# Start of a two-layer encoder trunk: the first token half loaded ahead of the rest, its squares summed by TensorE, and rows of 1/sqrt made without diagonals

## The chip, the cores and the metric

The kernel runs on one core of a Trainium2 chip. The metric is the device time of one execution in microseconds (us), the median of several runs. Engines are named as in the profile: PE (TensorE matmul), PEld (its weight loads), DVE (VectorE), ACT (ScalarE), POOL (GpSimd), SP (SyncE, which only issues transfers). A q behind a name is that engine's instruction queue.

## What is computed

Two layers of a hybrid encoder on 1024 tokens of 1024 channels, in float32:

```python
def rmsnorm(x, g):
    y = x * lax.rsqrt(jnp.mean(x * x, axis=-1, keepdims=True) + EPS)
    return y * g

for l in range(DEPTH):                                  # DEPTH = 2
    h = rmsnorm(x, attn_norm_g[l])
    x = x + hybrid_mixer(h, w_in[l], b_in[l], ...)      # z = h @ w_in + b_in; three branches, gates, w_out
    h = rmsnorm(x, ffn_norm_g[l])
    x = x + conv_ffn(h, w_up[l], ffn_conv_w[l], w_down[l])
return rmsnorm(x, final_norm_g)
```

The change touches the five rmsnorms (two in each layer and the last), the first one above all.

## The kernel before

Channels lie on the 128 partitions, tokens on the free axis. x is held as 8 channel tiles; the 1024 tokens are cut in two halves of 512 (h = 0, 1). Four transfers of 512 KB bring one half: transfer j brings channel tiles j and j + 4 (`x_load`). The input is x_i_0_0 to x_i_0_3 (first half) and x_i_1_0 to x_i_1_3 (second half).

The float32 products are made of float32r matmuls. Each operand is split into a high part (a cast, on ACT) and a low part (a subtraction, on DVE), and three matmuls make one product: high by high, weights' high by activations' low, weights' low by activations' high (`mms`, L336). Weights come as `raw` tiles of 256 KB with five buffers, and their two parts lie in `split` tiles (L286 on ACT, L287 on DVE).

Pairs of output tiles and both token halves make a 2 by 2 block product with one product saved (class `Block`). What this needs: B11 and B21 are the split parts of the normalised first half, T1 to T4 are sums and differences of both halves, s1 to s4 sums of weight quarters that accumulating transfers of the POOL queue make in DRAM-to-SBUF adds. `first` of a block needs the first half alone; `second` needs T2, and so the second half. `start_phase` runs `first` of four blocks, among which the second half's norm is made, then T2, then `second` of the four. So each phase (m_0 and m_1 for the mixers of layers 0 and 1, f_0 and f_1 for their FFNs) begins with the first half's norm.

An rmsnorm of a half: ACT squares each tile of x, DVE adds the eight squares up, PE sums over the partitions with four matmuls against a column of ones (`st`, one column for each 128 tokens), DVE makes the variance (`var`), POOL its power of -0.5 (`rs`, tokens on partitions, four columns). To have this as a row on all partitions, DVE splits it in a high and a low part (`rp`), multiplies the identity by each column (`dg`, two times 128x512), and PE multiplies ones by the two diagonals (`r`, two matmuls of 512 columns). DVE then multiplies x by the norm's weight and by r, eight times 128x512 (L479).

The order on each engine isn't that of the source. A scheduling layer orders the instructions with estimated times and sets the waits on semaphores. A transfer issued by SP or ACT signals one of eight semaphores, DMAHW0 to DMAHW7, given out in turn; before an issuing queue issues a transfer it waits until the transfer that had that semaphore before has landed, so at most eight are under way. `tc.issue_after(i)` keeps what is issued inside it behind instruction i. Before, SP alone issues all plain loads, in this order: four tiles of x's first half, the parameters (`par`, 195 KB), raw_0 to raw_2, four tiles of the second half, s2 of four blocks, raw_3 on.

Of the kernel before, what the change touches and what calls it, by code (L numbers as in the profile page):

```python
# [10 lines left out]
AF = mybir.ActivationFunctionType  # L11
ALU = mybir.AluOpType

P = 128
# [3 lines left out]
H = 512  # L18
NH = S // H
DB = 768  # L20
# [10 lines left out]
NB = H // BLK  # L31
# [70 lines left out]
def encoder(ctx: ExitStack, tc: tile.TileContext, xt, wts, par, bs, wst, cnt, out):  # L102
    nc = tc.nc
# [9 lines left out]
    def slot(name):  # L113

        return up.tile([P, 2, H], F32R, tag="u", name=name)
# [5 lines left out]
    def temp(name):  # L121
        return wp.tile([P, H], F32, tag="t", name=name, bufs=N_TT)
# [4 lines left out]
    def half(h):  # L127
        return slice(h * H, (h + 1) * H)

    parts = [const.tile([P, N_PAR], F32, name=f"par_{l}") for l in range(L)]  # L130
    ones = const.tile([P, P], F32, name="ones")
    nc.gpsimd.memset(ones, 1.0)
    ones_r = const.tile([P, P], F32R, name="ones_r")
    nc.vector.tensor_copy(ones_r, ones)
    ident = const.tile([P, P], F32, name="ident")
# [49 lines left out]
    raws, sums, split = {}, {}, {}  # L185
    state = {"raw": 0, "split": 0, "used": 0, "dma": None, "credit": 0, "pow": None}

    def load_to(n):
        while state["raw"] < min(n, len(raw_units)):
            i = state["raw"]  # L190
            l, t, c0, c1 = raw_units[i]
            w = wp.tile([P, H], F32, tag="raw", name=f"raw_{i}", bufs=N_RAW)
            ins = nc.sync.dma_start(w[:, : c1 - c0], wts[l, t, :, c0:c1])
            state["dma"] = ins.ins
            raws[i] = (w, c1 - c0)
            state["raw"] += 1

    def reload(dst, src):

        with tc.issue_after(state["dma"]):  # L200
            nc.sync.dma_start(dst, src)
# [47 lines left out]
    for l in range(L):  # L249
        plan_blocks(l, [in_tiles(*b) for b in IN_BLOCKS])  # L250
        for i in range(4):
            t, n = T_MIX + i // 2, NPP // 2 * P
# [90 lines left out]
    def halves(u, f):  # L343

        nc.scalar.copy(u[:, 0], f)  # L345
        nc.vector.tensor_tensor(u[:, 1], f, u[:, 0].bitcast(F32), op=ALU.subtract)
# [14 lines left out]
    def add(o, a, b, op=ALU.add):  # L361
        nc.vector.tensor_tensor(o, a, b, op=op)  # L362
# [45 lines left out]
            return run  # L408


    def rsqrt_sums(ss, c0, nc_, n, name):

        nb = nc_ // P
        st = pst.tile([P, H], F32, tag="st", name=f"st_{name}")
        for b in range(nb):
            nc.tensor.matmul(
                st[:, b : b + 1], ss[:, c0 + b * P : c0 + (b + 1) * P], ones[:, 0:1],
                start=True, stop=True,
            )
        var = sm.tile([P, NB], F32, tag="var", name=f"var_{name}")  # L420
        nc.vector.tensor_scalar(var[:, :nb], st[:, :nb], 1.0 / n, EPS, op0=ALU.mult, op1=ALU.add)
        rs = sm.tile([P, NB], F32, tag="rs", name=f"rs_{name}")
        state["pow"] = nc.gpsimd.tensor_tensor(
            rs[:, :nb], var[:, :nb], mhalf[:, :nb], op=ALU.pow
        ).ins
        rp = sm.tile([P, 2, NB], F32R, tag="rp", name=f"rp_{name}")
        nc.vector.tensor_copy(rp[:, 0, :nb], rs[:, :nb])
        nc.vector.tensor_tensor(
            rp[:, 1, :nb], rs[:, :nb], rp[:, 0, :nb].bitcast(F32), op=ALU.subtract
        )  # L430
        dg = wp.tile([P, 2, H], F32R, tag="dg", name=f"dg_{name}", bufs=1)
        for j in range(2):
            nc.vector.tensor_tensor(
                dg[:, j, :nc_].rearrange("p (b t) -> p b t", t=P),
                ident[:, None, :].broadcast_to([P, nb, P]),
                rp[:, j, :nb].bitcast(F32)[:, :, None].broadcast_to([P, nb, P]),
                op=ALU.mult,
            )
        return dg, nc_

    def rsqrt_rows(parts_of, name):

        dg, nc_ = parts_of
        r = pst.tile([P, H], F32, tag="st", name=f"r_{name}")
        for j in range(2):
            nc.tensor.matmul(r[:, :nc_], ones_r, dg[:, j, :nc_], start=j == 0, stop=j == 1)
        return r


    x_dram = [dp.tile([P, KD, S], F32, name=f"x_{i}") for i in range(2 * L)]  # L450

    def x_load(src, h, name, gated=True):

        xq = []
        for j in range(4):
            t = up.tile([P, 2, H], F32, tag="u", name=f"x_{name}_{j}")
            s = src[:, j::4, half(h)]
            if gated:
                reload(t, s)
            else:  # L460
                nc.sync.dma_start(t, s)
            xq.append(t)
        return xq

    def x_part(xq, k):
        return xq[k % 4][:, k // 4]

    def square(sq, xq, k, cols, name):

        s = temp(f"sq_{name}_{k}")  # L470
        nc.scalar.activation(s[:, cols], x_part(xq, k)[:, cols], AF.Square)
        if sq is None:
            return s
        add(sq[:, cols], sq[:, cols], s[:, cols])
        return sq
# [20 lines left out]
    def start_phase(l, col, x0, x1, sq1, name, ops, blocks, late):  # L496
# [3 lines left out]
        for b in blocks[:at]:  # L500
            b.first()
        rows = rsqrt_sums(sq1, 0, H, D, f"{name}_1")
        blocks[at].first()
        r = rsqrt_rows(rows, f"{name}_1")
        for b in blocks[at + 1 :]:
            b.first()
# [214 lines left out]
    def mixer_out(l, d, x_src, x_dst):  # L721
        pr = parts[l]
        tag = f"{l}"
        ws, q = layer[l]

        def col(c):
            return pr[:, c : c + 1]
# [11 lines left out]
        def mix_weights(n):  # L739
            t, at = n // per, n % per * P  # L740
            key = (l, T_MIX + t, at // H * H)
            if key not in wm:
                wm[key] = operand("raw", key)
            return wm[key], at % H

        for m in range(KB):
# [3 lines left out]
            for h in range(NH):  # L750
                ps = pm.tile([P, H], F32, tag="mm", name=f"mix_{tag}_{m}_{h}")
                for n in mine:
                    w, at = mix_weights(n)
# [65 lines left out]
        conv, squares = [], []  # L819
# [27 lines left out]
        def conv_norm():  # L847
            for h in range(NH):
                sl = half(h)
                dg = rsqrt_sums(squares[h], 0, H, DB, f"c_{tag}_{h}")  # L850
                yield
                r = rsqrt_rows(dg, f"c_{tag}_{h}")
                for i in range(KB):
                    c = conv[i][:, sl]
                    nc.vector.tensor_tensor(c, c, r, op=ALU.mult)
                    s = temp(f"csg_{tag}_{h}_{i}")
                    nc.scalar.activation(
                        s, c, AF.Sigmoid, bias=col(C_CLB + i), scale=col(C_CLG + i)
                    )
                    nc.scalar.activation(  # L860
                        c, c, AF.Identity, bias=col(C_CLB + i), scale=col(C_CLG + i)
                    )
                    nc.vector.tensor_tensor(c, c, s, op=ALU.mult)
                    a[h][i] = slot(f"a_{tag}_{h}_{i}")
                    halves(a[h][i], c)
                    yield
# [31 lines left out]
        branch(2, mixed, PUMP[1])  # L898
        drain()
        background.append(conv_norm())  # L900
        branch(1, us, PUMP[2])
        drain()
        branch(0, a, 0)

        def out_half(h, hook):
            xq = x_load(x_src, h, f"o_{l}_{h}")
            sq = None
            for m in range(KD):
                ps = pm.tile([P, H], F32, tag="mm", name=f"po_{tag}_{m}_{h}")
                for j in range(2):  # L910
                    w = operand("raw", (l, T_OUT + m, j * H))
                    mms(ps, w, y[h][j * 4 : j * 4 + 4], j == 0, j == 1)
                xm = x_part(xq, m)
                add(xm, ps, xm)
                nc.sync.dma_start(x_dst[:, m, half(h)], xm)
                sq = square(sq, xq, m, slice(0, H), f"f_{l}_{h}")
                if m == 0 and hook is not None:
                    hook()
            return xq, sq

        x0, sq0 = out_half(0, None)
# [5 lines left out]
        x1, sq1 = out_half(1, hook)  # L927
        return x0, x1, sq1, ops

    def first_half(l, col, x0, sq0, name):  # L930
        normed(x0, rsqrt_rows(rsqrt_sums(sq0, 0, H, D, f"{name}_0"), f"{name}_0"), l, col)
        return first_operands(x0, name)
# [137 lines left out]
            nc.sync.dma_start(out[:, k : k + each, h * H + cols.start : h * H + cols.stop], fv)  # L1070


    x0 = x_load(xt, 0, "i_0", gated=False)
    nc.sync.dma_start(parts[0], par[0])
    load_to(3)
    x1 = x_load(xt, 1, "i_1", gated=False)
    warm = sm.tile([P, 1], F32, tag="warm", name="warm", bufs=1)
    nc.scalar.activation(warm, ones[:, 0:1], AF.Sigmoid)
    sq0 = sq1 = None
    for k in range(KD):  # L1080
        sq0 = square(sq0, x0, k % 2 * 4 + k // 2, slice(0, H), "m_0_0")
    ops = first_half(0, C_NG, x0, sq0, "m_0")
    for k in range(KD):
        sq1 = square(sq1, x1, k % 2 * 4 + k // 2, slice(0, H), "m_0_1")
# [3 lines left out]
    for l in range(L):  # L1088
        x_src = xt if l == 0 else x_dram[2 * l - 1]
        d = mixer_in(l, x0, x1, sq1, ops)  # L1090
        x0, x1, sq1, ops = mixer_out(l, d, x_src, x_dram[2 * l])
        if l + 1 < L:
            x0, x1, sq1, ops = ffn(l, x0, x1, sq1, ops, x_dram[2 * l], x_dram[2 * l + 1])
# [96 lines left out]
```

## Time and profile before

| | |
|---|---|
| median of 3 runs | 2747.4 us (2745.45 to 2749.69) |
| profiled execution, its own time | 2748.52 us |
| its span in the profile | 2746.8 us |
| granted TensorE clock, mean | 0.996 |
| PE busy | 2682.3 us (98% of the span) |
| DVE, ACT, POOL busy | 2057.0, 1255.1, 359.1 us |
| on the chain that ended last | PE 80%, "issue" 7%, DVE 6%, transfers 4%, ACT 1% |

A row of the timeline gives the start in us, the time until the end of the last of its instructions, engine, source line, operation, out<-in, how many instructions, and in brackets the idle time of that engine before it with what ended it. A row of a waits view names who waited for whom: us in total, times, longest. Rows of a windows view give busy us of each engine in one stretch. Tile names there have no numbers: x_i is either half, sq_m its squares. One float32 matmul of the source shows as two rows on PE, a float32r one as one.

### The profile page before, as it was taken

What the parts mean: (1) busy time and instruction counts of PE and PEld (TensorE: products, weight loads), DVE (VectorE), ACT (ScalarE), POOL (GpSimd) and SP (SyncE); (2) the same over time, 40 slices, a digit from 0 to 9 for tenths busy, and PEclk for the clock granted to TensorE, in tenths of its full rate; (3) what the DMA queues carried; (4) which work ended last, traced back from release to release, by engine and by line L of the source; (5) the groups of instructions that cost most, each with busy time, mean ns of one, the idle gap of its engine ahead of it and who ended that gap; (6) DMA issues with size and microseconds to landing.
All of it is one profiled execution on the core that took longest, in us unless ns stands there. A gap on an engine that the chain in (4) does not pass through costs nothing.

```text
span 2746.8 us, 35054 instructions
## 1 busy us (share of the span) xinstructions
PE 2682.3 (98%) x12122; PEld 2209.9 (80%) x12122; DVE 2057.0 (75%) x2899; ACT 1255.1 (46%) x2059; POOL 359.1 (13%) x411
## 2 busy tenths in 40 slices
PE   6999999999999999999999999999999999999998
PEld 4887888878888788878888878888778887888788
DVE  7978879967756876674589789899586579666656
ACT  5654444443333555453365444444352336445534
POOL 2212111100001221100122111110000022211000
PEclk9999999999999999999999999999999999999999
DMA  8887787675357787655568777875634677774654
GB/s 236 200 207 190 206 225 197 185 265 174 112 182 203 169 207 178 172 200 199 150 152 213 195 210 213 217 198 193 230 125 137 205 188 182 198 179 121 215 177 138
DMA packets 272003, 517.92 MB, mean 189 GB/s; under 512 B 28496, under 2 KB 49744, under 8 KB 271824
## 3 DMA queue, kind: packets, MB, share of 16 engines
q1 hardware_dynamic: 217200, 415.51, 45.4%
q0 software_dynamic: 54624, 100.16, 22.2%
q8 instruction: 95, 1.56, 0.2%
q14 instruction: 84, 0.69, 0.1%
HBM read 385.54 MB, written 89.13 MB: 173 GB/s over the span
## 4 chain that ended last, share of the span: by engine, by line
PE 80%; issue 7%; DVE 6%; DMA 4%; ACT 1%; POOL 0%; SPq 0%; DVEq 0%; POOLq 0%; ACTq 0%
PE run_up L336 12%; PE pd L336 12%; PE run_gate L336 10%; PE c_up L336 9%; PE ph L336 9%; PE c_gate L336 7%; PE po L336 4%; PE run_glu L336 4%; PE c_glu L336 3%; DVE conv L590 2%; PE run_v L336 2%; PE c_v L336 2%; PE run_zp L336 1%; DMA poold<-pooled 1%; PE mix L336 1%
## 5 line engine op out<-in xcount | busy, mean ns | idle before, releaser
L286 ACT CAST split<-raw 128x512 fp32r<-128x512 f32 (+1 forms) x570 | 342.8, 603 | 474.2 <-PE ph L336 155.6
L287 DVE TENSOR_TENSOR split<-raw,split 128x512 fp32r<-128x512 f32 (+1 forms) x570 | 376.5, 664 | 226.5 <-ACT split L286 222.9
L590 DVE SCALAR_TENSOR_TENSOR conv<-z_glu,par,conv 128x1023 f32<-128x1023 f32 (+9 forms) x360 | 451.8, 1262 | 10.4 <-ACT conv L588 8.3
L286 ACT CAST split<-s 128x512 fp32r<-128x512 f32 x344 | 213.4, 622 | 352.7 <-issue 115.2
L336 PE MATMUL pd<-h,split 128*128 128x512 f32 (+1 forms) x1536 | 314.2, 363 | 3.4 <-ACT split L286 1.5
L336 PEld LDWEIGHTS pd<-h,split 128*128 128x128 f32 x1536 | 262.0, 188 | 51.1 <-ACT h L358 3.0
L287 DVE TENSOR_TENSOR split<-s,split 128x512 fp32r<-128x512 f32 x344 | 234.7, 685 | 71.2 <-ACT split L286 70.4
L218 POOL DMA_DIRECT2D s<-in_wts_dram x220 | 204.5, 968 | 427.7 <-DMA s<-in_wts_dram 202.3
L218 POOL DMA_DIRECT2D s<-s x156 | 135.7, 870 | 762.3 <-DMA s<-in_wts_dram 366.0
L336 PE MATMUL run_up<-T_f,split 128*128 128x512 f32 x768 | 184.5, 389 | 2.5 <-ACT T_f L345 2.5
L336 PE MATMUL run_up<-B_f,split 128*128 128x512 f32 x768 | 182.0, 391 | 2.3 <-DVE upv L362 2.3
L336 PE MATMUL c_up<-T_f,split 128*128 128x512 f32 x768 | 183.8, 389 | 0.3 <-ACT p_up L398 0.3
L336 PE MATMUL po<-y,split 128*128 128x512 f32 x768 | 175.7, 389 | 0.0
L336 PEld LDWEIGHTS run_up<-B_f,split 128*128 128x128 f32 x768 | 143.3, 188 | 34.4 <-DVE upv L362 4.6
L336 PEld LDWEIGHTS run_up<-T_f,split 128*128 128x128 f32 x768 | 143.8, 188 | 33.5 <-ACT T_f L345 3.3
L336 PEld LDWEIGHTS c_up<-T_f,split 128*128 128x128 f32 x768 | 144.0, 188 | 31.0 <-ACT p_up L398 1.2
L336 PEld LDWEIGHTS po<-y,split 128*128 128x128 f32 x768 | 144.0, 188 | 29.8
L336 PE MATMUL c_gate<-T_m,split 128*128 128x512 f32 x576 | 138.4, 389 | 0.0
L336 PE MATMUL run_gate<-T_m,split 128*128 128x512 f32 x576 | 138.4, 389 | 0.0
L336 PE MATMUL run_gate<-B_m,split 128*128 128x512 f32 x576 | 135.6, 389 | 0.0
L336 PE MATMUL ph<-mixed,split 128*128 128x512 f32 x576 | 135.3, 393 | 0.0
L336 PE MATMUL ph<-us,split 128*128 128x512 f32 x576 | 134.2, 391 | 0.0
(256 smaller groups left out, 4388.0 us busy)
## 6 DMA issues: line engine op xcount, KB each, us to landing
raw<-in_wts_dram SPq DMA_DIRECT2D x518, 256.0 KB, 3.4
s<-in_wts_dram SPq DMA_DIRECT2D x344, 256.0 KB, 3.6
s<-in_wts_dram POOLq DMA_DIRECT2D x220, 256.0 KB, 5.2
s<-s POOLq DMA_DIRECT2D x156, 256.0 KB, 4.1
gate<-z_gate SPq DMA_DIRECT2D x48, 512.0 KB, 4.2
gt<-gate SPq DMA_DIRECT2D x96, 256.0 KB, 3.8
h<-hd SPq DMA_DIRECT2D x56, 256.0 KB, 4.6
poold<-pooled SPq DMA_DIRECT2D x24, 512.0 KB, 4.7
```

The costliest lines, as they stand in the source:

```text
L218: nc.gpsimd.dma_start(s, o, accum_op=ALU.add)
L286: nc.scalar.copy(s[:, 0, :cols], src[:, :cols])
L287: nc.vector.tensor_tensor(s[:, 1, :cols], src[:, :cols], s[:, 0, :cols].bitcast(F32), op=ALU.subtract)
L336: nc.tensor.matmul(ps[:, cols], w[:, i0, wsl], a[:, i1, cols], start=first and k == 0 and j == 0, stop=last and k == n - 1 and j == 2, ski ...
L590: nc.vector.scalar_tensor_tensor(acc[:, k:], ain[:, : S - k], col(w0 - k), acc[:, k:], op0=ALU.mult, op1=ALU.add,)
```

## The change

Three things change.

1. Issue of the first loads. SP issues x's first half and goes on to s2 and raw_3. ACT's queue issues par, raw_0 to raw_2 and x's second half, behind the square of the second part of x_i_0_0.
2. Sums of the first half's squares. No DVE adds; PE runs its four matmuls with the ones for each of the eight squares, accumulating in `st`.
3. Rows of 1/sqrt. In all rmsnorms `rp` and `dg` go; four float32 matmuls of 128 columns take a column of `rs`, broadcast to 128x128, as weights and the identity as moving operand. The convolution's layernorm (`conv_norm`) keeps its diagonals.

```diff
-    def load_to(n):
+    def load_to(n, queue=nc.sync):
...
-            ins = nc.sync.dma_start(w[:, : c1 - c0], wts[l, t, :, c0:c1])
-            state["dma"] = ins.ins
+            ins = queue.dma_start(w[:, : c1 - c0], wts[l, t, :, c0:c1])
+            if queue is nc.sync:
+                state["dma"] = ins.ins
...
-    def rsqrt_sums(ss, c0, nc_, n, name):
+    def rsqrt_sums(ss, c0, nc_, n, name, diagonals=False):
...
-        for b in range(nb):
-            nc.tensor.matmul(
-                st[:, b : b + 1], ss[:, c0 + b * P : c0 + (b + 1) * P], ones[:, 0:1],
-                start=True, stop=True,
-            )
+        if not isinstance(ss, list):
+            ss = [ss]
+        for i, s in enumerate(ss):
+            for b in range(nb):
+                nc.tensor.matmul(
+                    st[:, b : b + 1], s[:, c0 + b * P : c0 + (b + 1) * P], ones[:, 0:1],
+                    start=i == 0 and b == 0, stop=i == len(ss) - 1 and b == nb - 1,
+                    skip_group_check=True,
+                )
...
+        if not diagonals:
+            return rs, nc_
...
     def rsqrt_rows(parts_of, name):
-        dg, nc_ = parts_of
+        rs, nc_ = parts_of
         r = pst.tile([P, H], F32, tag="st", name=f"r_{name}")
+        if rs.shape[-1] == NB:
+            for b in range(nc_ // P):
+                nc.tensor.matmul(
+                    r[:, b * P : (b + 1) * P], rs[:, b : b + 1].broadcast_to([P, P]), ident,
+                    start=True, stop=True,
+                )
+            return r
...
-    x0 = x_load(xt, 0, "i_0", gated=False)
-    nc.sync.dma_start(parts[0], par[0])
-    load_to(3)
-    x1 = x_load(xt, 1, "i_1", gated=False)
+    x0 = x_load(xt, 0, "i_0", nc.sync)
...
-    sq0 = sq1 = None
+    sq0, sq1 = [], None
     for k in range(KD):
-        sq0 = square(sq0, x0, k % 2 * 4 + k // 2, slice(0, H), "m_0_0")
+        s = (load_tile if k < 2 else temp)(f"sq_m_0_0_{k}")
+        arrived = nc.scalar.activation(s, x_part(x0, k % 2 * 4 + k // 2), AF.Square)
+        sq0.append(s)
+        if k == 1:
+            with tc.issue_after(arrived.ins):
+                nc.scalar.dma_start(parts[0], par[0])
+                load_to(3, nc.scalar)
+                x1 = x_load(xt, 1, "i_1", nc.scalar)
```

What the scheduling layer makes of it, on ACT at the program's start. Before, the squares of the first half (sq_m_0_0) stand together and the first weight casts right behind them:

```order
L471 ACTIVATE sq_m_0_0_2_132<-x_i_0_2_100 128x512 [waits DMAHW2_49]
L471 ACTIVATE sq_m_0_0_6_135<-x_i_0_2_100 128x512
L471 ACTIVATE sq_m_0_0_3_138<-x_i_0_3_102 128x512 [waits DMAHW3_49,DVE_49]
L471 ACTIVATE sq_m_0_0_7_141<-x_i_0_3_102 128x512 [waits DVE_49]
L286 CAST split_0_280<-raw_0_105 128x512 [waits DMAHW5_49]
L286 CAST split_1_283<-raw_1_107 128x512 [waits DMAHW6_49]
```

Now eight issues stand between the second square and the third, four of them with a wait on a semaphore:

```order
L1094 ACTIVATE sq_m_0_0_1_108<-x_i_0_0_96 128x512
L1099 DMA par_0_78<-in_par_dram 128x390
L193 DMA raw_0_111<-in_wts_dram 128x512
L193 DMA raw_1_113<-in_wts_dram 128x512
L193 DMA raw_2_115<-in_wts_dram 128x512
L476 DMA x_i_1_0_117<-in_xt_dram 128x2x512 [waits DMAHW2_49]
L476 DMA x_i_1_1_119<-in_xt_dram 128x2x512 [waits DMAHW5_49]
L476 DMA x_i_1_2_121<-in_xt_dram 128x2x512 [waits DMAHW0_49]
L476 DMA x_i_1_3_123<-in_xt_dram 128x2x512 [waits DMAHW3_49]
L1094 ACTIVATE sq_m_0_0_2_125<-x_i_0_1_98 128x512 [waits DMAHW1_49]
L1094 ACTIVATE sq_m_0_0_3_127<-x_i_0_1_98 128x512
```

The holders before them: x_i_1_0 follows x_i_0_2 on DMAHW2, x_i_1_1 follows raw_0 on DMAHW5, x_i_1_2 follows raw_2 on DMAHW0, and x_i_1_3 follows s2_0_14 on DMAHW3, which SP issues and which itself follows par_0 there. SP's rows now:

```order
L476 DMA x_i_0_3_102<-in_xt_dram 128x2x512
L210 DMA s2_0_1_281<-in_wts_dram 128x512
L210 DMA s2_0_12_285<-in_wts_dram 128x512 [waits DMAHW1_49]
L210 DMA s2_0_14_289<-in_wts_dram 128x512 [waits DMAHW3_49]
L210 DMA s2_0_24_293<-in_wts_dram 128x512 [waits DMAHW4_49]
L193 DMA raw_3_306<-in_wts_dram 128x512 [waits DMAHW6_49]
```

So s2 and raw_3 stand where par, raw_0 to raw_2 and the second half stood.

On DVE, before, the low parts of the first weights are made ahead of the first half's norm (x_i by r_m) or between its steps:

```order
L287 TENSOR_TENSOR split_0_280<-raw_0_105,split_0_280 128x512
L421 TENSOR_SCALAR var_m_0_0_149<-st_m_0_0_144 128x4
L287 TENSOR_TENSOR split_1_283<-raw_1_107,split_1_283 128x512
L427 CAST rp_m_0_0_153<-rs_m_0_0_151 128x4
L428 TENSOR_TENSOR rp_m_0_0_153<-rs_m_0_0_151,rp_m_0_0_153 128x4
L433 TENSOR_TENSOR dg_m_0_0_156<-ident_84,rp_m_0_0_153 128x512 x2
L287 TENSOR_TENSOR split_2_286<-raw_2_109,split_2_286 128x512
L479 SCALAR_TENSOR_TENSOR x_i_0_0_96<-x_i_0_0_96,par_0_78,r_m_0_0_159 128x512
```

Now they come behind the eight norm steps and the eight low parts of B11 and B21, one in turn with each sum of the second half's squares (sq_m_0_1):

```order
L347 TENSOR_TENSOR B21_m_0_3_208<-x_i_0_3_102,B21_m_0_3_208 128x512
L363 TENSOR_TENSOR sq_m_0_1_0_211<-sq_m_0_1_0_211,sq_m_0_1_1_216 128x512
L288 TENSOR_TENSOR split_0_297<-raw_0_111,split_0_297 128x512
L363 TENSOR_TENSOR sq_m_0_1_0_211<-sq_m_0_1_0_211,sq_m_0_1_5_219 128x512
L288 TENSOR_TENSOR split_1_300<-raw_1_113,split_1_300 128x512
L363 TENSOR_TENSOR sq_m_0_1_0_211<-sq_m_0_1_0_211,sq_m_0_1_2_222 128x512
```

The cast of split_0 on ACT moved likewise, from ahead of the first B11 cast to behind the sixth of the eight B casts. On PE, ten matmuls of the first blocks that need no low part of a weight now stand ahead of the first that does (three before).

More of the change, by code (lines that the diff above doesn't have):

```diff
@@ L441, in rsqrt_rows, with x_load @@
     def rsqrt_rows(parts_of, name):
-        dg, nc_ = parts_of
+        rs, nc_ = parts_of
         r = pst.tile([P, H], F32, tag="st", name=f"r_{name}")
+        if rs.shape[-1] == NB:
[5 more added lines that the diff above has]
+            return r
         for j in range(2):
-            nc.tensor.matmul(r[:, :nc_], ones_r, dg[:, j, :nc_], start=j == 0, stop=j == 1)
+            nc.tensor.matmul(r[:, :nc_], ones_r, rs[:, j, :nc_], start=j == 0, stop=j == 1)
         return r
     x_dram = [dp.tile([P, KD, S], F32, name=f"x_{i}") for i in range(2 * L)]
-    def x_load(src, h, name, gated=True):
+    def x_load(src, h, name, queue=None):
         xq = []
@@ L457, in x_load @@
             s = src[:, j::4, half(h)]
-            if gated:
+            if queue is None:
                 reload(t, s)
             else:
-                nc.sync.dma_start(t, s)
+                queue.dma_start(t, s)
             xq.append(t)
@@ L849, in conv_norm @@
                 sl = half(h)
-                dg = rsqrt_sums(squares[h], 0, H, DB, f"c_{tag}_{h}")
+                dg = rsqrt_sums(squares[h], 0, H, DB, f"c_{tag}_{h}", True)
                 yield
```

## The prediction

> **What bounds the kernel now.** First the page's busy line, then a windows view that cuts the span at 26, 62 and 2738 us (busy us of each engine, with the number of instructions), then the waits of PE over the whole span.
>
> ```profile
> PE 2682.3 (98%) x12122; PEld 2209.9 (80%) x12122; DVE 2057.0 (75%) x2899; ACT 1255.1 (46%) x2059; POOL 359.1 (13%) x411
> ```
>
> ```profile
> core 0: us, PE busy (x) PEld busy (x) DVE busy (x) ACT busy (x) POOL busy (x), PEclk, DMA share, GB/s
> 0.00:26.00 26.00, 5.25 (x13) 3.15 (x13) 14.30 (x25) 14.61 (x26) 5.09 (x12) 1.00 0.93 315
> 62.00:2738.00 2676.00, 2643.12 (x11980) 2180.21 (x11980) 2008.65 (x2815) 1223.29 (x2005) 340.58 (x383) 1.00 0.67 187
> 2738.00:2747.00 9.00, 0.82 (x2) 0.56 (x2) 3.48 (x8) 1.78 (x5) 0.69 (x1) 0.57 0.35 117
> ```
>
> ```profile
> PE st_m L416 <- DVE sq_m L362: 14.3, 1, 14.3
> PE run_glu L336 <- ACT T_m L345: 3.5, 3, 2.2
> PE run_up L336 <- ACT T_f L345: 2.5, 2, 1.2
> PE r_fin L446 <- DVE dg_fin L433: 1.9, 1, 1.9
> ```
>
> From 62 to 2738 us PE works for 2643 of 2676 us: nothing that other engines save there shortens the kernel, unless PE waits for it. PE is idle at the two ends: 20.8 of the first 26 us and 8.2 of the last 9. So the change is worth what it moves the start of PE's work, plus what it takes from the last chain, plus what it adds to PE between. The start is read from the timeline, and the landings from SP's rows, because a queue waits for an earlier landing before it issues:
>
> ```profile
> 0.74 2.61 SPq L461 DMA_DIRECT2D x_i<-in_xt_dram  x4
> 4.70 1.15 ACT L471 ACTIVATE sq_m<-x_i 128x512 f32<-128x512 f32 x2 [2.48 <-DMA x_i<-in_xt_dram]
> 8.78 1.15 ACT L471 ACTIVATE sq_m<-x_i 128x512 f32<-128x512 f32 x2 [2.93 <-DMA x_i<-in_xt_dram]
> 11.53 1.15 ACT L471 ACTIVATE sq_m<-x_i 128x512 f32<-128x512 f32 x2 [0.27 <-DMA x_i<-in_xt_dram]
> 14.26 1.84 PE L416 MATMUL st_m<-ones,sq_m 128*128 128x1 f32 x8 [14.26 <-DVE sq_m L362]
> 16.13 0.16 DVE L421 TENSOR_SCALAR var_m<-st_m 128x4 f32<-128x4 f32 x1 [1.42 <-PE st_m L416]
> 17.82 0.17 DVE L427 CAST rp_m<-rs_m 128x4 fp32r<-128x4 f32 x1 [0.92 <-POOL rs_m L423]
> 20.28 5.36 DVE L479 SCALAR_TENSOR_TENSOR x_i<-x_i,par,r_m 128x512 f32<-128x512 f32 x8 [0.28 <-PE r_m L446]
> 25.55 4.90 DVE L346 TENSOR_TENSOR B_m<-x_i,B_m 128x512 fp32r<-128x512 f32 x8
> 26.29 5.06 PE L336 MATMUL run_glu<-B_m,split 128*128 128x512 f32 x11 [0.60 <-DVE B_m L346]
> 30.37 0.68 DVE L362 TENSOR_TENSOR sq_m<-sq_m,sq_m 128x512 f32<-128x512 f32 x1
> 30.97 0.68 DVE L287 TENSOR_TENSOR split<-raw,split 128x512 fp32r<-128x512 f32 x1
> 31.15 3.33 PE L336 MATMUL c_glu<-B_m,split 128*128 128x512 f32 x11
> 34.32 2.67 PE L336 MATMUL run_v<-B_m,split 128*128 128x512 f32 x11
> 41.59 0.95 PE L416 MATMUL st_m<-ones,sq_m 128*128 128x1 f32 x8
> 46.20 1.10 PE L446 MATMUL r_m<-dg_m,ones_r 128*128 128x512 f32 x2
> ```
>
> The chain: the last x tile of the half at 11.53, squares, sums on DVE, PE's st at 14.26, var, rs, rp and dg, r, the norm's eight steps from 20.28, the low parts B_m from 25.55, and with the first of these PE runs without a break from 26.29.
>
> **Part 1: ACT issues loads, and waits.** The two squares of the first tile end at 5.85. Then ACT issues par and three raws, and four x tiles of which each waits for a semaphore: for x_i_0_2, raw_0, raw_2, and last for s2_0_14. What is queued behind these on ACT is the other six squares of the first half, and everything after them. So the norm cannot begin before s2_0_14, a weight sum that nothing needs yet, has landed. SP issues that one only when par has landed, since they share a semaphore. "Loaded alone" isn't what happens either: s2_0_1 follows x at once on SP, and ACT's loads begin with three quarters of x outstanding. When does s2_0_14 land?
>
> ```profile
> x_i<-in_xt_dram SPq DMA_DIRECT2D x8, 512.0 KB, 7.9
> raw<-in_wts_dram SPq DMA_DIRECT2D x13, 256.0 KB, 6.8
> par<-in_par_dram SPq DMA_DIRECT2D x2, 195.0 KB, 7.4
> 13.98 0.34 SPq L209 DMA_DIRECT2D s<-in_wts_dram  x1
> 15.33 0.33 SPq L193 DMA_DIRECT2D raw<-in_wts_dram  x1
> 16.69 0.33 SPq L193 DMA_DIRECT2D raw<-in_wts_dram  x1
> ```
>
> By their semaphores these three SP rows mark the landing of raw_2, x_i_1_0 and x_i_1_1, that is of 3011, 3523 and 4035 KB in the order of before: 512 KB in 1.36 us. Ahead of s2_0_14's end come at least x's half, par and three s2 (2048 + 195 + 768 = 3011 KB): 14.0 us. With ACT's raws too it is 3779 KB: 15.33 + 256/512 x 1.36 = 16.0. With two of the x tiles as well, 4803 KB: 16.69 + 768/512 x 1.36 = 18.7; with all three that can be issued, 5315 KB: 20.1. I take the middle of the two inner values, 17.4, because raws and x tiles go out earlier than s2_0_14 but on another queue; ends 14.0 and 20.1. [...]
>
> **Part 2: sums on PE instead of DVE.** ACT's issue of x_i_1_3 takes 2.61/4 = 0.65, so it squares again from 18.1. The first of six is done 0.63 later (18.7), the others every 0.52. Each now has its own four float32 matmuls, eight rows as in st_m: 1.84 us on a PE that had been idle (14.26), and 0.95 on one at full pace (41.59), of which some 0.8 in a stream. PE reached its pace slowly when it started: eleven rows took 5.06, then 3.33, then 2.67 us. So I take three groups slow and three fast: 3 x 1.84 + 3 x 0.8 = 7.9, until 26.6; ends 4.8 (all fast) and 11.0 (all slow). The seven DVE adds that go were hidden by nothing before, but they no longer matter: the squares come later than any add did. [...]
>
> From the end of st to rs it is 17.82 - 16.10 = 1.7: 28.3.
>
> **Part 3: rows without diagonals.** This float32 form is not in the trace; its nearest rows are sv's 128x128 float32 matmuls.
>
> ```profile
> 601.57 2.08 PE L795 MATMUL sv<-ws,v 128*128 128x128 f32 x22
> 900.11 1.29 DVE L433 TENSOR_TENSOR dg_f<-ident,rp_f 128x512 fp32r<-128x512 f32 x2
> 903.54 0.63 PE L446 MATMUL r_f<-dg_f,ones_r 128*128 128x512 f32 x2
> 916.31 8.95 PE L336 MATMUL run_up<-T_f,split 128*128 128x512 f32 x38 [1.23 <-ACT T_f L345]
> 2737.19 0.58 PE L416 MATMUL st_fin<-ones,sq_n 128*128 128x1 f32 x4 [1.58 <-DVE sq_n L362]
> 2738.83 0.17 DVE L427 CAST rp_fin<-rs_fin 128x2 fp32r<-128x2 f32 x1 [0.87 <-POOL rs_fin L423]
> 2740.61 2.48 DVE L1067 TENSOR_TENSOR fin<-fin,r_fin 128x512 f32<-128x512 f32 x4 [0.74 <-PE r_fin L446]
> ```
>
> 22 such rows take 2.08, so eight take 0.76 and with the last one's end 1.0; on a slow PE as st, 1.84. I take 1.0, since PE has just summed. The norm's first step then stands at 29.3 instead of 20.28: 9.0 later. (Before, rp, dg and r took 2.4 here.)
>
> In the middle of the kernel the shorter chain is worth nothing where r stands in its place on PE anyway: in f_0, dg is done at 901.4 and r runs at 903.54, behind a block's matmuls. So I leave the waits for T2 (2.5 in both FFNs, 0.8 of run_glu's 3.5 in m_1, all 3.3) as they are; lower end, all gone. PE pays 0.76 instead of 0.47 for an r, 0.3 each at four places where it doesn't wait next (f_0, m_1, f_1 and the last norm, first halves): +1.2. At the very end rp, dg and r, 1.78 from 2738.83 to 2740.61, become four float32 rows, 0.6 as st_fin, and a hand-over: -1.1.
>
> **Part 4: the low parts of the weights.** From the norm's first step DVE needs 5.27 (20.28 to 25.55) and 4.82 for the eight B_m (to 30.37), and only then, by the new order, 0.60 for a sum of squares and 0.69 for split_0's low part: 11.4 us. PE's first unbroken run needs that part. Before, it began 26.29 - 20.28 = 6.0 behind the first step, the splits being there. So 5.4 more. Ten matmuls instead of three lie ahead of it: seven, at 0.24 (run_v) to 0.46 (run_glu), 1.6 to 3.2; I take 2.4 off. The cover that is gone: the splits were made while DVE waited for r.
>
> What follows hangs on PE: r_m of the second half stands behind 72 matmuls of the first blocks, before at 46.20 and now as much later as the run began. T2 follows it on DVE as before; r itself is 0.2 shorter. raw_5 to raw_7 wait for the buffers that the late splits free, from 40.7 on; a raw lands 6.8 after issue, at 47.5, and PE needs the fifth only after four blocks, beyond 50.
>
> **The sum.** Norm +9.0, low parts +5.4, ten matmuls ahead -2.4, so PE's run and r_m begin 12.0 later; second r -0.2; r in the middle +1.2; end -1.1: +11.9. The profiled execution took 2748.5 us and so would take 2760.4; the median of the runs shown is 1.1 lower: 2759.3.
>
> **Rivals.**
> - *Faster: x arrives sooner and ACT isn't held.* If the tiles came every 1.36 us behind the first (4.70), the fourth would be there at 8.8 instead of 11.53; squares to 10.0, last sums 0.8, rs 1.7, r 1.0: 13.6, which is 6.7 earlier. With +5.4, -2.4, -0.2, +1.2, -1.1 that gives -3.8, and with the T2 waits gone -7.1: 2740.3. Against it: ACT's four waits in the order. The chain from s2_0_14's landing to the first step takes 11.9 (17.4 to 29.3), so the change is even only with a landing at 5.5, and at 8.6 if all sums are fast. par is issued after 5.85, and a transfer took 6.8 or more at the median.
> - *No change.* s2_0_14 at 14.0 (-3.4), sums all fast (-3.1), the seven early matmuls worth 3.2 (-0.8), T2 waits gone (-3.3): +1.3, 2748.7. It takes nearly all of these to come within 5.5 us.
> - *Slower still.* Transfer at 20.1 (+2.7), sums all slow (+3.1), r slow (+0.8): +18.5, 2765.9.
>
> **How the numbers follow.** About 0.2%, 5.5 us, is what a measurement of this kernel can tell from no change. My forecast, ACT held until s2_0_14 has landed and PE late by 6 to 16 us, has 0.70; the slower case 0.15; no change 0.11; faster 0.04. So slower 0.85, same 0.11, faster 0.04. The time is the likeliest case's, 2759.3. The range leaves out the faster case and half of the no-change one below (from 2750.5) and the far end of the slow case above (to 2766).
>
> **What would show it.** ACT's third square near 18 us with a wait ahead of it, behind SP's or ACT's issues; st_m spread over 7 to 8 us; the norm's first step near 29; DVE's split_0 behind all B_m, near 40; the long run_glu row near 41; T2's first matmul near 67 instead of 55.37; at the end the first fin row 0.7 us behind rs instead of 1.8. The forecast is wrong if the six squares run before 14 us, if split_0's low part is ready when B_m is, or if PE stands still later for something that the late start had hidden.

## The result, and the profile after

| | before | after |
|---|---|---|
| median (four runs each, side by side) | 2746.43 us | 2760.85 us |
| ratio, 95% interval | | 1.0055 [1.0041, 1.0068] |
| profiled execution, its span | 2748.52, 2746.8 us | 2760.40, 2757.5 us |

The change makes the kernel 0.55% slower, some 15 us. First the page's busy line and two rows of PE's waits, after the change:

```profile
PE 2696.4 (98%) x12236; PEld 2228.1 (81%) x12236; DVE 2038.2 (74%) x2848; ACT 1255.8 (46%) x2059; POOL 361.2 (13%) x411
PE st_m L421 <- ACT sq_m L1094: 14.7, 2, 9.1
PE run_glu L337 <- ACT split L287: 5.6, 1, 5.6
```

The DVE work that went and the PE work that came hardly show in the shares. The second wait shows the new order: ahead of the first blocks PE waits for the weights' high parts, for which run_glu had no wait before. The start is told by the timeline:

```profile
9.73 7.80 ACTq L476 DMA_DIRECT2D x_i<-in_xt_dram  x4
17.58 3.22 ACT L1094 ACTIVATE sq_m<-x_i 128x512 f32<-128x512 f32 x6 [11.54 <-DMA x_i<-in_xt_dram]
18.26 10.40 PE L421 MATMUL st_m<-ones,sq_m 128*128 128x1 f32 x48 [9.05 <-ACT sq_m L1094]
28.70 0.16 DVE L427 TENSOR_SCALAR var_m<-st_m 128x4 f32<-128x4 f32 x1 [27.50 <-PE st_m L421]
30.40 2.08 PE L455 MATMUL r_m<-ident,rs_m 128*128 128x128 f32 x8 [1.74 <-POOL rs_m L429]
32.52 5.36 DVE L494 SCALAR_TENSOR_TENSOR x_i<-x_i,par,r_m 128x512 f32<-128x512 f32 x8 [3.06 <-PE r_m L455]
37.79 4.90 DVE L347 TENSOR_TENSOR B_m<-x_i,B_m 128x512 fp32r<-128x512 f32 x8
43.21 0.68 DVE L288 TENSOR_TENSOR split<-raw,split 128x512 fp32r<-128x512 f32 x1
43.95 2.56 PE L337 MATMUL run_glu<-B_m,split 128*128 128x512 f32 x10 [0.39 <-DVE split L288]
46.35 2.43 PE L337 MATMUL c_glu<-B_m,split 128*128 128x512 f32 x10
59.09 1.05 PE L455 MATMUL r_m<-ident,rs_m 128*128 128x128 f32 x8
67.74 0.50 PE L337 MATMUL run_glu<-T_m,split 128*128 128x512 f32 x1 [1.68 <-ACT T_m L346]
```

ACT's row of four issues lasts until 17.53, and only then, at 17.58, do the six other squares begin: the 11.54 us of idle time in the bracket were waits of ACT's own queue. Then 48 sums on PE for 10.40 us, the norm's first step at 32.52 (before 20.28), split_0's low part behind all eight B_m, PE's unbroken run from 43.95 (before 26.29), T2's first matmul at 67.74 (before 55.37): 12.4 later. The last rows:

```profile
2750.36 0.87 PE L455 MATMUL r_fin<-ident,rs_fin 128*128 128x128 f32 x4 [1.10 <-POOL rs_fin L429]
2751.33 2.48 DVE L1082 TENSOR_TENSOR fin<-fin,r_fin 128x512 f32<-128x512 f32 x4 [1.81 <-ACT fin L1078]
```

From r_fin's release, where rs is done, to the first fin row it is 1.0 us; before it was 1.8 (2738.80 to 2740.61).

The span is 10.7 longer, though T2 stood 12.4 later. One difference lies right behind T2. A windows view of PE there (busy us, rows, granted clock, DMA share, GB/s), first before, then after:

```profile
56.40:59.70 3.30, 3.30 (x9) 0.50 0.96 151
```

```profile
67.70:71.10 3.40, 3.34 (x13) 1.00 0.94 133
```

Before, PE ran these 3.3 us at half clock and after it did not, which is worth some 1.7 us, an estimate from half of 3.3. What lies behind T2 thus differs from one trace to another by a us or two, and a place in one trace is not the gain of the whole.

### The profile page after: what moved, and what is told of

Same layout as the page of the kernel before. It is cut to its first block, busy times and chain, and to the rows that moved or that the text cites. A ratio compares the mean times of both kernels' runs of the same rounds, so it can differ in the third digit from the quotient of the medians.

```text
span 2757.5 us, 35248 instructions
## 1 busy us (share of the span) xinstructions
PE 2696.4 (98%) x12236; PEld 2228.1 (81%) x12236; DVE 2038.2 (74%) x2848; ACT 1255.8 (46%) x2059; POOL 361.2 (13%) x411
## 4 chain that ended last, share of the span: by engine, by line
PE 80%; issue 8%; DVE 6%; DMA 4%; ACT 1%; POOL 0%; SPq 0%; DVEq 0%; POOLq 0%; ACTq 0%
PE run_up L337 12%; PE pd L337 11%; PE run_gate L337 9%; PE c_up L337 9%; PE ph L337 9%; PE c_gate L337 7%; PE po L337 4%; PE run_glu L337 4%; PE c_glu L337 3%; PE run_v L337 2%; DVE conv L605 2%; PE c_v L337 2%; PE run_zp L337 1%; DMA poold<-pooled 1%; PE mix L337 1%
```

## Experiments

Each ratio is against the kernel before, run on the same chip at the same time, with its 95% interval; a difference in us is that ratio times the median of before there (2743.5 to 2744.7). Traces are compared with the one trace of before, in which x's last tile was squared from 11.53 us on; in the kernels below that load x in the same way it came at 10.25 to 10.95, so about 1 us of a shift against that trace is its own.

**One part at a time: the loads alone.**

```diff
 # before, with
+    x0 = x_load(xt, 0, "i_0", nc.sync)
...
+        if k == 1:
+            with tc.issue_after(arrived.ins):
+                nc.scalar.dma_start(parts[0], par[0])
+                load_to(3, nc.scalar)
+                x1 = x_load(xt, 1, "i_1", nc.scalar)
```

> The kernel before with the first loads issued as in the changed kernel, par, three weight units and x's second half from ACT's queue, and nothing else: DVE adds the squares, diagonals stay. The prediction's Part 1 alone. My theory: ACT is held as in the changed kernel, its third square near 17.4, the last of the adds near 22.5, the eight st rows 1.8, var and rs 1.7, rp, dg and r 2.5: the norm's first step near 28.4 (+8), T2's first matmul near 63.5, the whole +8. Rival: ACT's hold comes only with the sums on PE, or is hidden by DVE's adds: first step below 22, no difference.

Measured: 2761.14 us, 1.0057 [1.0045, 1.0070], 15.6 us more than before. The loads alone cost as much as the whole change, and twice the +8 I had written. The timeline:

```profile
8.84 8.24 ACTq L462 DMA_DIRECT2D x_i<-in_xt_dram  x4
17.12 3.23 ACT L1080 ACTIVATE sq_m<-x_i 128x512 f32<-128x512 f32 x6 [11.14 <-DMA x_i<-in_xt_dram]
22.61 1.84 PE L417 MATMUL st_m<-ones,sq_m 128*128 128x1 f32 x8 [22.61 <-DVE sq_m L363]
24.48 0.16 DVE L422 TENSOR_SCALAR var_m<-st_m 128x4 f32<-128x4 f32 x1 [1.42 <-PE st_m L417]
26.77 0.31 POOL L536 MEMSET ws<- 64x256 f32 x1 [25.32 <-DMA ws<-in_wst_dram]
27.16 1.03 POOL L424 TENSOR_TENSOR rs_m<-var_m,mhalf 128x4 f32<-128x4 f32 x1
31.16 5.36 DVE L480 SCALAR_TENSOR_TENSOR x_i<-x_i,par,r_m 128x512 f32<-128x512 f32 x8 [0.29 <-PE r_m L447]
67.50 0.50 PE L337 MATMUL run_glu<-T_m,split 128*128 128x512 f32 x1 [1.68 <-ACT T_m L346]
```

The hold is the same (squares from 17.12). The sums on DVE end 4.2 us sooner than those on PE did (st done at 24.45 instead of 28.66), but 2.4 of it is lost at once: var is done at 24.64, and rs begins at 27.16 (in the changed kernel 0.16 behind var), since POOL's queue has a memset of ws ahead of it that waits for a transfer. I had not expected that wait; the first step stands at 31.16 instead of the 28.4 I wrote. T2 is 12.1 later than before, not 8: my +8 also left out that the loads move the weights' low parts behind B_m here too. The 3.5 between T2 and the 15.6 of the medians are not explained. The rival, that the hold comes only with the sums on PE, falls.

**The sums on PE alone, and the rows alone.**

```diff
 # before, with (sums)
+        sq0.append(s)
 # before, with (rows, in all five rmsnorms)
+                nc.tensor.matmul(
+                    r[:, b * P : (b + 1) * P], rs[:, b : b + 1].broadcast_to([P, P]), ident,
+                    start=True, stop=True,
+                )
```

> The kernel before with the eight squares of the first half summed on PE, and nothing else: SP loads and diagonals stay. The prediction's Part 2 alone. With the loads on SP the sums ended at 19.46, near 7 us behind the last square, and the rows without diagonals were worth nothing, so the norm's first step stands near 23.5 (4 to 5 later than with DVE's sums) and the whole 5 to 7 us above the kernel before. Rival: PE's catching up in the first blocks hides the delay: within 2 us.

> The kernel before with the rows of 1/sqrt made without diagonals in all five rmsnorms, and nothing else: DVE sums and SP loads stay. The prediction's Part 3 alone: at the head rp, dg and r (2.5 us from the end of rs to the first step) become eight rows on a slow PE (2.1), -0.3; at the end -0.8; in the middle +0.3 at four places, +1.2: in all +0.1, no difference. Rival: in the four kernels run so far the medians lie 4 to 6 us further above the kernel before than their T2 does, so the rows in the middle cost 4 us or more that a single trace hides: +3 to +5.

Measured: sums 2745.22 us, 1.0004 [0.9995, 1.0013]; rows 2745.24 us, 1.0005 [0.9996, 1.0014]. First the sums' timeline, then that of the rows:

```profile
10.87 1.15 ACT L1097 ACTIVATE sq_m<-x_i 128x512 f32<-128x512 f32 x2 [0.20 <-DMA x_i<-in_xt_dram]
5.53 13.79 PE L421 MATMUL st_m<-ones,sq_m 128*128 128x1 f32 x64 [5.53 <-ACT sq_m L1097]
23.19 5.35 DVE L494 SCALAR_TENSOR_TENSOR x_i<-x_i,par,r_m 128x512 f32<-128x512 f32 x8 [0.29 <-PE r_m L461]
57.13 0.50 PE L337 MATMUL run_glu<-T_m,split 128*128 128x512 f32 x1 [1.79 <-ACT T_m L346]
```

```profile
10.47 1.15 ACT L485 ACTIVATE sq_m<-x_i 128x512 f32<-128x512 f32 x2 [0.26 <-DVE sq_m L362]
18.66 5.36 DVE L493 SCALAR_TENSOR_TENSOR x_i<-x_i,par,r_m 128x512 f32<-128x512 f32 x8 [2.45 <-PE r_m L454]
54.59 0.50 PE L336 MATMUL run_glu<-T_m,split 128*128 128x512 f32 x1 [1.75 <-ACT T_m L345]
```

With the sums on PE the chain of sums, not x, ends last: 64 rows in 13.79 us, until 19.32, 7.3 behind the last square. From the end of the last square to the first step it takes 11.2 us instead of 7.6, yet T2 stands only 2.5 behind that of the rows kernel, and the whole is 1.1 us (-1.4 to +3.6) above before. My 5 to 7 was too much: of the 4.5 us between the first steps of these two kernels 2.0 are caught up at T2. The rows cost 1.4 us (-1.1 to +3.8), which the prediction's +0.1 fits; of the rival's 3 to 5 the lower end is not excluded.

**Undoing the loads.** The first kernel puts all loads back on SP and keeps sums and rows; the second puts only x's second half back on SP, so that ACT issues nothing that waits.

```diff
 # after, with (first)
+    nc.sync.dma_start(parts[0], par[0])
+    load_to(3)
+    x1 = x_load(xt, 1, "i_1", nc.sync)
 # after, with (second)
+    x1 = x_load(xt, 1, "i_1", nc.sync)
...
-                x1 = x_load(xt, 1, "i_1", nc.scalar)
```

> The changed kernel with every load back on SP's queue, in the order of the kernel before: ACT issues nothing and squares each x tile as it lands. The sums on PE and the rows without diagonals stay. My theory: what made the change slow is ACT held for a landing, and then slow float32 sums on PE. Without the hold the first square of x's last tile ends near 12.7 us as before, but the eight groups at 1.73 us are a chain of their own from 9.4 us to near 19.8; the norm's first step near 23.7 (before 20.3, changed 32.5), T2's first matmul near 59, the whole 9 us below the changed kernel, about 2751. Rival 1, the sums cost nothing once ACT is free (groups of 0.8): first step near 16.4, the whole near 2744. Rival 2, the hold was not the cost (the sums and the late low parts are): first step above 28, the whole within 4 us of the changed kernel.

> The changed kernel with x's second half alone issued by SP again, behind the first half; par and the first three weight units stay on ACT, which then has no issue that waits. My theory (the hold is in those four issues): squares run as x lands, the last near 13; the sums at 1.73 us a group end near 19.5, the norm's first step near 23.3, split_0's low part 11.4 behind it at 34.7, the whole 9 us below the changed kernel, near 2751. Rival: it is the crowding of the queues, not the hold, that makes x late: x's last tile lands after 13 us as now or later, first step above 26. With the low parts worth 3 us net, as the prediction had it, this kernel is 3 us behind the one with all loads on SP; with them worth nothing, the two agree within 1 us.

Measured: 2751.03 us, 1.0026 [1.0014, 1.0037], and 2752.41 us, 1.0028 [1.0019, 1.0038]: half of the loss is gone in both. The two timelines, one behind the other:

```profile
5.68 13.78 PE L421 MATMUL st_m<-ones,sq_m 128*128 128x1 f32 x64 [5.68 <-ACT sq_m L1097]
23.33 5.36 DVE L494 SCALAR_TENSOR_TENSOR x_i<-x_i,par,r_m 128x512 f32<-128x512 f32 x8 [3.05 <-PE r_m L455]
56.92 0.50 PE L337 MATMUL run_glu<-T_m,split 128*128 128x512 f32 x1 [1.68 <-ACT T_m L346]
```

```profile
10.58 1.15 ACT L1095 ACTIVATE sq_m<-x_i 128x512 f32<-128x512 f32 x2 [0.80 <-DMA x_i<-in_xt_dram]
23.23 5.36 DVE L494 SCALAR_TENSOR_TENSOR x_i<-x_i,par,r_m 128x512 f32<-128x512 f32 x8 [3.06 <-PE r_m L455]
58.67 0.50 PE L337 MATMUL run_glu<-T_m,split 128*128 128x512 f32 x1 [1.88 <-ACT T_m L346]
```

In the second kernel ACT still issues par and three weight units, and x's last tile is squared from 10.58, as early as with SP alone. So it is the four issues that wait which hold ACT. This kernel also takes x's second half off ACT's queue, so it does not by itself rule out that crowding made x late; but in the changed kernel the last of the four was issued at 16.99, and behind it the six squares then ran without a wait (3.22 us). The first step stands where I put it (23.3), 9.2 us earlier than in the changed kernel. What stays open: sums and rows together, loads on SP, cost 7.1 us (3.8 to 10.2), while alone they cost 1.1 and 1.4. T2 does not tell them apart (56.92 and 57.13), so the rest lies somewhere behind it, or in the scatter, for the intervals are wide: from T2 to the end of the span it is 2695.5 us in the trace of the one (span 2752.4) and 2688.5 in that of the sums alone (span 2745.6).

**The low parts of the weights.**

```diff
 # after, with
+    split_to(3)
     ops = first_half(0, C_NG, x0, sq0, "m_0")
```

> The changed kernel with the first three weight units split ahead of the first half's norm instead of behind it: DVE makes their low parts while it waits for r, and PE has three matmuls ahead of its run instead of ten. ACT is held as in the changed kernel, so the first step stays at 32.5. The prediction's Part 4: the late low parts cost 5.4 less 2.4, so 3.0 us come back (near 2757.8). Rival, read from the two traces: T2's first matmul stands 35.1 us behind the first step before and 35.2 after, so the late low parts cost nothing, since PE catches up at its full pace: within 1 us of the changed kernel (2760 to 2761). In both, PE's run begins near 38.5 instead of 43.95.

Measured: 2761.16 us, 1.0055 [1.0038, 1.0071], no gain that can be told. In the timeline PE's run and T2's first matmul:

```profile
38.26 4.55 PE L337 MATMUL run_glu<-B_m,split 128*128 128x512 f32 x11 [0.46 <-DVE B_m L347]
65.84 0.72 PE L337 MATMUL run_glu<-T_m,split 128*128 128x512 f32 x1 [2.09 <-ACT T_m L346]
```

PE's run starts 5.7 us earlier, but slow: eleven matmuls in 4.55 us, where the late run made ten in 2.56. At T2 the gain is 1.9, and right behind it this trace has a stretch of half clock that the changed kernel's lacks (in the same windows view):

```profile
66.00:69.30 3.30, 3.30 (x8) 0.50 0.97 153
```

That can take back what was won, some 1.7 us by the same estimate. The pair with x on SP agrees on the price up to T2: from the first step to T2 it is 33.6 us with split_0 early and 35.4 with all splits late. So the late low parts cost 1.6 to 1.9 us there, neither the 3.0 of the prediction nor nothing; in the medians neither pair shows it clear of the noise.

**What makes PE slow.** The changed kernel with PE made to work ahead of the sums. The expectation below says that the first three weight units are split early here too; this kernel makes them late (first low part at 41.4), so it is read against the changed one.

```diff
 # after, with
+    busy = pm.tile([P, H], F32, tag="mm", name="busy")
+    for _ in range(56):
+        nc.tensor.matmul(
+            busy.rearrange("p (b t) -> p b t", t=P), ones_r,
+            ones_r[:, None, :].broadcast_to([P, NB, P]), start=True, stop=True,
+        )
     ops = first_half(0, C_NG, x0, sq0, "m_0")
```

> The changed kernel with 56 matmuls of ones (128x512, result unused) ahead of the sums on PE, which is idle there: about 16 us of work from 1.2 us. The first three units are split early here too, so it is read against the kernel with the early splits. Theory: the sums and r are slow because PE has not been working, whatever they read: the 48 rows of six groups fall from 10.4 to 5 or less behind squares that come every 0.6 us (so the sums end with the last square, near 22.5), r from 2.08 to 1.05, and the norm's first step stands near 25.5 instead of 32.5; the whole 6 to 7 us below the early splits. Rival 1: float32 sums of one column are slow by their kind at this place (weights loaded anew for each): rows unchanged, first step near 32.5 or later, no gain. Rival 2: the matmuls of ones also run slow throughout (26 us), and the sums wait behind them: first step at 36 or later.

Measured: 2759.92 us, 1.0053 [1.0036, 1.0070], no gain that can be told where I had written 6 to 7 us. Rows of the timeline, then a windows view of PE (its busy us, rows, granted clock, DMA share, GB/s):

```profile
1.25 15.38 PE L1104 MATMUL busy<-ones_r 128*128 128x512 f32 x56 [1.25 <-DVE ones_r L134]
16.46 10.42 PE L421 MATMUL st_m<-ones,sq_m 128*128 128x1 f32 x64
28.62 2.08 PE L455 MATMUL r_m<-ident,rs_m 128*128 128x128 f32 x8 [1.74 <-POOL rs_m L429]
```

```profile
18.00:20.00 2.00, 2.00 (x20) 1.00 0.97 295
20.00:22.00 2.00, 2.00 (x11) 0.50 1.08 387
```

And one row of the same view of the changed kernel:

```profile
20.00:22.00 2.00, 2.00 (x11) 1.00 1.05 396
```

This is the reading of the case. The counts in brackets take in rows that only reach into a stretch: by their starts 18 rows begin in the 2 us before 20, a row each 0.11 us, and 9 in the 2 us behind, one each 0.21. The granted clock falls from 1.00 to 0.50 at the same moment, 3.4 us after the last wide matmul (16.63), while PE is 100% busy with the sums. So in this trace the slow rows go with the clock, and 3.4 us of float32 sums of one column, at 100% busy, did not keep it at 1.00. The theory was right on the cause and wrong on the size: I had taken the sums themselves for work that holds the clock. r, at 28.62, was slow again (2.08 us), and the first step stood at 30.74 instead of the 25.5 I wrote. Faster sums alone could not have reached it: here as with the loads alone POOL's memset of ws stood ahead of rs, until 26.99.

The 3.4 us are not the same in every trace: in the kernel with 36 fillers below, the clock fell 4.6 us after the last wide matmul (12.27 to 16.9), with PE idle for 1.75 of them. And in the changed kernel, where no wide matmul stood ahead of the sums, all 48 rows were slow: 10.40 us.

**What is left over.** Loads on SP as before, DVE adds six squares and PE sums three tiles (that sum and the last two squares), the first three weight units split early, rows without diagonals at the first and the last norm, once without and once with fillers whose result isn't used:

```diff
 # with fillers
+    for _ in range(36):
+        nc.tensor.matmul(
+            busy.rearrange("p (b t) -> p b t", t=P), ones_r,
+            ones_r[:, None, :].broadcast_to([P, NB, P]), start=True, stop=True,
+        )
     ops = first_half(0, C_NG, x0, sq0, "m_0")
+    for _ in range(12):
+        nc.tensor.matmul(busy, ones_r, ops["B11"][0][:, 0], start=True, stop=True)
```

> What the runs so far leave over, without help for PE: loads on SP as before, DVE adds six squares and PE sums three tiles (that sum and the last two squares), splits of the first three weight units early, rows without diagonals only at the first norm and the last, diagonals between. Three groups of sums on a PE that has not worked: 1.73 each from 12.0 to 17.2, rs 18.9, r 2.1: first step near 21 (before 20.3), the end 0.8 shorter: no difference (-1 to +1). Rival: the fewer DVE steps pay at once, first step near 18.5, -3.

> The same kernel with matmuls on PE that compute nothing used: 36 of 512 columns of ones from 1.25 us until x's squares come, and 12 on the first cast tile ahead of the first block. Theory: PE's clock follows matmuls of many columns; the three groups then take 0.7 each, st ends near 13.5, rs 15.2, r about 1.1 to 1.6, first step near 16.7 (3.6 earlier than before), and PE's first blocks run at full pace instead of slow for 7 us (3 us more): -4 to -7 against the kernel before, 4 or more below the same kernel without them. Rival: the 12 matmuls ahead of the blocks delay PE's run by as much as its pace gives back, or the blocks are paced by DVE's low parts: -3 or less.

Measured: without fillers 2747.04 us, 1.0005 [0.9997, 1.0014]; with them 2743.87 us, 0.9991 [0.9982, 1.0000]. Without, then with:

```profile
11.41 5.25 PE L421 MATMUL st_m<-ones,sq_m 128*128 128x1 f32 x24 [11.41 <-DVE sq_m L363]
```

```profile
12.10 2.74 PE L421 MATMUL st_m<-ones,sq_m 128*128 128x1 f32 x24
16.59 1.80 PE L455 MATMUL r_m<-ident,rs_m 128*128 128x128 f32 x8 [1.75 <-POOL rs_m L429]
51.64 0.79 PE L337 MATMUL run_glu<-T_m,split 128*128 128x512 f32 x1 [3.25 <-ACT T_m L346]
```

```profile
16.00:17.00 1.00, 0.41 (x3) 0.96 1.05 389
17.00:18.00 1.00, 1.00 (x7) 0.50 1.05 385
```

The same 24 rows take half the time. But by the windows view (the second fence with fillers) the clock fell 0.3 us after r began, and ahead of T2 PE now waits 3.25 us for a cast. The gain is 2.5 us (0 to 4.9), at the median less than the 4 to 7 I wrote. I took that cast for one that waits for DVE; ACT's rows of the same trace say otherwise:

```profile
49.84 0.62 ACT L287 CAST split<-s 128x512 fp32r<-128x512 f32 x1 [3.47 <-DMA s<-in_wts_dram]
50.98 0.60 ACT L346 CAST T_m<-x_i 128x512 fp32r<-128x512 f32 x1
```

The row of T2's cast has no idle time in front of it: it stands on ACT behind the cast of a weight sum, which waited 3.47 us for its landing. With an earlier start it is that landing which ends last ahead of T2.

The next kernel puts two float32 fillers of 512 columns between st and r, and makes the second half's row without diagonals as well, which frees DVE of a dg (1.29 us for dg_f before):

```diff
+            for q in sq0[1:]:
+                nc.tensor.matmul(filler, ones, q, start=True, stop=True)
...
+        rows = rsqrt_sums(sq1, 0, H, D, f"{name}_1", name != "m_0")
```

> The kernel with filler matmuls, with two changes: two float32 fillers of 512 columns stand between st and r, so that r comes while PE's clock is still high, and the second half's norm of the first mixer has its row without diagonals, since DVE now is what PE waits for there (3.25 us ahead of T2). Theory: r 1.05 instead of 1.80, first step near 17.7 instead of 18.43, dg's 1.3 us of DVE gone ahead of T2, so T2's first matmul near 49.5 instead of 51.64: 2 us below the kernel with fillers, -4 to -5 against the kernel before. Rival: r begins later, behind the fillers, or T2 waits for something else on DVE: no better than the kernel with fillers, -1 to -3.

Measured: 2739.15 us, 0.9980 [0.9972, 0.9989], 5.5 us less than before (3.0 to 7.7): faster than the kernel before and the changed one. Its timeline:

```profile
15.06 1.96 PE L951 MATMUL filler<-sq_m,ones 128*128 128x512 f32 x4
16.95 1.16 PE L455 MATMUL r_m<-ident,rs_m 128*128 128x128 f32 x8
50.60 0.50 PE L337 MATMUL run_glu<-T_m,split 128*128 128x512 f32 x1 [2.71 <-ACT T_m L346]
```

r takes 1.16 instead of 1.80, and T2 comes 1.0 earlier than with the first fillers. That is by as much as the weight sum's cast starts earlier (48.80, behind a wait of 2.94 for its landing, instead of 49.84), so a freer DVE is not shown to have brought it. The two edits were not tried alone, the medians differ by more than T2 does, and their intervals overlap: that this kernel beats the one with the first fillers is likely but not shown.

## Why the prediction was right, point by point

The median came out at 2760.85, 1.6 us above the 2759.3 forecast, within the range. The mechanism was right; two terms of the sum were too small, one too large, and these nearly cancelled, so the closeness of the time is in part luck. Taken as a difference, +11.9 stands against some 15.

- **ACT held (Part 1): right.** Squares again from 17.58; the prediction had 18.1. ACT's last issue, which waits for s2_0_14, came at 16.99, where the prediction had taken 17.4 for that landing. Taken alone, the loads carry the whole loss.
- **Sums on PE (Part 2): too small.** Three groups slow and three fast, 7.9 us, became 10.40: all six slow, at 1.73. The step that was off is "PE reached its pace slowly when it started", taken over from 512-column matmuls to matmuls of one column.
- **r (Part 3): too small.** 1.0 was 2.08, for the same reason; "since PE has just summed" was the wrong way round. With both terms the first step came at +12.2 instead of +9.0.
- **Low parts (Part 4): the order right, the price too high.** split_0's low part was done 11.4 behind the first step (32.52 to 43.89), as worked out. But what the seven early matmuls were worth was more than the 2.4 for their time: PE was at full pace when its run began. That the early matmuls brought it there was not tried. Ten matmuls of run_glu and ten of c_glu took 2.56 and 2.43 us, before eleven and eleven 5.06 and 3.33. From the first step to r_m of the second half it was 26.6 us after and 25.9 before, 0.7 more instead of 3.0.
- **r in the middle, and the end.** The rows alone cost 1.4 (-1.1 to +3.8), head and end taken in, so the +1.2 of the middle can't be told from nothing. The end gave 0.8, not 1.1; the profile names ACT's fin, not r, as what released the first fin row.
- **The sum.** +12.0 at PE's run and r_m became +12.9 at r_m and +12.4 at T2, where the prediction named a time near 67: 67.74.
- **Terms in a row are not parts to be undone one by one.** The sum adds hold, sums, rows and low parts along one chain, but the loads alone already cost as much as all together: without the sums on PE, DVE's adds and a memset on POOL took their place on the chain.
- **The rivals.** "Faster" needed ACT free: with it free, x's last tile was squared from 10.58, and the kernel was still 7.7 us slower than before: the first step stood at 23.23 behind slow sums, and the low parts came late. What each of these is worth stays open, since the sums alone cost 1.1. "No change" needed all sums fast, among other things. "Slower still" had the sums and r nearly right, and the transfer too late.

## What to carry to other kernels

Four transfers issued by ACT put their waits for landings in front of its squares, 11.54 us of idle time: read in the order what each issue waits for before moving issues off SP. A cast that waited for a landing did the same: on ACT one of a weight sum, after 3.47 us of waiting, held the cast that PE's T2 needed. Sums by matmuls of one column were cheap here only behind wide matmuls: 24 rows took 2.74 us behind fillers and 5.25 on a PE that had been idle. On such a PE count them at twice the price, or put wide matmuls around them. And a part that is cheap alone can take the place of another on the chain, so a change of several parts is told apart only by running each part alone and each left out.

## What was not expected of the hardware

- PE was 100% busy by the profile, with float32 matmuls of one column, and its granted clock still fell to 0.50, 3.4 us after the last matmul of 512 columns (4.6 in another trace); a row then began every 0.21 us instead of every 0.11.
- Two float32 matmuls of 512 columns (four rows, 1.96 us) between st and r went with a granted clock of 1.00 through r, where it had fallen to 0.50 without them: r took 1.16 us instead of 1.80.
- At the start of these traces the granted clock reads 1.00 while PE is slow: the changed kernel's sums ran at 4.6 rows per us with 1.00 shown, the pace that had 0.50 beside it behind the fillers. So at the start I went by the pace of the rows, not by that column; that the clock was low there is inferred from the pace alone.
